# Index scores of two query blocks on ScalarE and GpSimd, weights' low parts in pieces, projection steps put first

## The chip, the cores and the metric

The kernel runs on one core of a Trainium2 chip. The metric is the device time of one execution in microseconds (us); the median of three runs of the kernel before is 1162.57 us (1162.12 to 1164.31). A difference below about 0.2%, some 2.3 us, can't be told from none.

## The reference

A trunk of two layers over 512 tokens of width 1024. Layer 0 mixes tokens with a sparse attention whose indexer picks keys (mixer A), layer 1 with a latent attention (mixer B); a squared-ReLU MLP follows each. Inputs and outputs are float32. What the change touches is mixer A's indexer:

```python
proj = h @ w_in                       # 16 heads of q, 4 of k and v, 8 index heads qi, one ki, weights wi
logits = einsum('bthd,bsd->bths', qib, ki)
score = einsum('bths,bth->bts', relu(logits), wib)   # sum over 8 index heads
score = where(visible, score, -inf)                  # chunks of 64, causal by chunk
_, sel = lax.top_k(score, 128)                       # keys that a query attends to
...                                                  # softmax attention of 16 heads over the selected keys
x = x + squared_relu_mlp(rms_norm(x), w_up, w_down)  # after each mixer; d_ff = 4096
```

## The kernel before

Every product of two float32 matrices is three TensorE passes on split numbers (a high part rounded to fp32r and a low part, the remainder): high by high, low by high, high by low, as `mm3` issues them (L227 to L229). So each weight tile is split before it is used. `Weights` keeps an ordered list of weight tiles ("items", mostly 128 partitions x 1024); `convert` fetches one with a DMA, makes the high part on ScalarE (L143, or on GpSimd at L141 for items marked "p" first) and the low part as raw minus high on GpSimd (L150, or on VectorE when so marked). MLP down weights go through L148 instead, which already works in pieces of 512 columns. Five items are held at a time, so a cast on ScalarE waits until TensorE is done with an item five earlier.

In mixer A, `idx_tile` projects the index queries and keys (`ip`, copied to `inat`), VectorE rotates 16 of every 64 columns (`rope`, L382, L384, L385) and scales the weights of heads (L741). `proj_tiles` is a generator of 32 steps, each three matmuls of 512 columns into a bank `pp`, that projects keys and values (`kv_done` copies them out on ScalarE and rotates on GpSimd) and then queries; `next(side)` puts one step between other work. After the index projection, TensorE transposes the rotated queries (`q_turn`, `qip`, L750) and keys (`kip`, L759), and these are split into `qis` and `ki`.

The index scores go over query blocks qb = 3, 2, 1 of 128 rows (block 0 needs no selection) with N = 512, 384, 256 keys, and for each over eight heads: one projection step, then two matmuls into a bank `lp` (L800, L801), then the sum over heads. Head 0 is max(x, 0) times its weight, straight from PSUM on VectorE (L804); heads 1 to 7 are a relu on ScalarE (L807) into one of two buffers and a multiply-add on VectorE into `bias` (L808). A memset masks the last chunk (L812). The scores of qb 3, 2, 1 stand in bias_120, bias_119, bias_118.

The selection (`rounds`) then takes 16 rounds per block on VectorE: MAX8 finds the eight largest (L777), MATCH_REPLACE8 marks them (L779), and at the end a compare turns marks into a mask of 0 and -1e30 (L781). Rounds of the blocks that are ready are taken in turn. The order of instructions on each engine is set by a scheduler from the written order and its own estimates; each engine then runs its list in order. The attention that follows adds `bias` to the scores in its row maximum on VectorE (L522).

In mixer B VectorE rotates the queries (L382, L384, L385 on `qn`, transposed by TensorE at L1021) while GpSimd makes both parts of the weights of later head groups (L141, L150).

## Time and profile before

| what | us |
|---|---|
| median of three runs | 1162.57 |
| the profiled execution's own time | 1162.26 |
| span of its trace | 1160.5 |
| TensorE busy (96% of the span) | 1116.6 |
| VectorE, ScalarE, GpSimd busy | 782.3, 604.3, 666.0 |

TensorE is busy nearly throughout, and its clock was granted in full but for a few stretches, so the time lies in the places where TensorE waits. They are in the first 16 us, in mixer A (to about 230 us), in mixer B (630 to 760 us) and in the last 10 us. Between these lie the two MLPs. A timeline row gives start, duration, engine, line, operation, output<-inputs and shape, and in brackets how long the engine had been idle and which instruction ended that.

### The profile page before, as it was taken

What the parts mean: (1) busy time and instruction counts of PE and PEld (TensorE: products, weight loads), DVE (VectorE), ACT (ScalarE), POOL (GpSimd) and SP (SyncE); (2) the same over time, 40 slices, a digit from 0 to 9 for tenths busy, and PEclk for the clock granted to TensorE, in tenths of its full rate; (3) what the DMA queues carried; (4) which work ended last, traced back from release to release, by engine and by line L of the source; (5) the groups of instructions that cost most, each with busy time, mean ns of one, the idle gap of its engine ahead of it and who ended that gap; (6) DMA issues with size and microseconds to landing.
All of it is one profiled execution on the core that took longest, in us unless ns stands there. A gap on an engine that the chain in (4) does not pass through costs nothing.

```text
span 1160.5 us, 15969 instructions
## 1 busy us (share of the span) xinstructions
PE 1116.6 (96%) x5721; PEld 949.8 (82%) x5721; DVE 782.3 (67%) x1419; ACT 604.3 (52%) x1115; POOL 666.0 (57%) x495
## 2 busy tenths in 40 slices
PE   6899899999999999999999899999999999999997
PEld 6778678879888888888889788888988888888886
DVE  7699998663566567566566888886556466556664
ACT  5453687654544554454445666563464454454452
POOL 4557433453657757856703642654457866856772
PEclk9999899999999999999999999999999999999999
DMA  6322100243124214313222200111414314412402
GB/s 210 111 64 86 67 1 2 72 135 103 63 83 145 91 55 145 127 55 110 80 66 79 75 31 25 55 55 55 164 56 145 109 56 126 146 56 90 145 12 80
DMA packets 65607, 99.56 MB, mean 86 GB/s; under 512 B 3188, under 2 KB 41848, under 8 KB 65528
## 3 DMA queue, kind: packets, MB, share of 16 engines
q1 hardware_dynamic: 65528, 98.55, 26.7%
q8 instruction: 45, 0.74, 0.3%
q14 instruction: 34, 0.28, 0.1%
HBM read 96.44 MB, written 2.10 MB: 85 GB/s over the span
## 4 chain that ended last, share of the span: by engine, by line
PE 79%; DVE 12%; issue 3%; ACT 3%; POOL 1%; DMA 1%; SPq 0%; DVEq 0%; POOLq 0%; ACTq 0%
PE dn L1144 22%; PE up L227 10%; PE up L228 10%; PE up L229 10%; PE s_ps L514 3%; PE o_ps L576 3%; PE wo_ps L227 2%; PE wo_ps L228 2%; PE wo_ps L229 2%; PE pt_ps L533 2%; DVE bias L779 2%; DVE m L777 2%; PE dn L228 1%; PE dn L229 1%; PE dn L227 1%
## 5 line engine op out<-in xcount | busy, mean ns | idle before, releaser
L148 POOL TENSOR_TENSOR w_lo<-quad,w_hi 128x512 fp32r<-128x512 f32 x196 | 275.0, 1433 | 162.9 <-ACT w_hi L143 160.3
L150 POOL TENSOR_TENSOR w_lo<-w_raw,w_hi 128x1024 fp32r<-128x1024 f32 (+4 forms) x117 | 265.0, 2284 | 89.0 <-ACT w_hi L143 88.6
L1147 DVE TENSOR_TENSOR x<-dn,x 128x512 f32<-128x512 f32 x196 | 135.0, 691 | 138.4 <-PE dn L1144 138.4
L228 PE MATMUL up<-hT_lo,w_hi 128*128 128x512 f32 (+1 forms) x576 | 210.5, 366 | 0.0
L227 PE MATMUL up<-hT_hi,w_hi 128*128 128x512 f32 (+1 forms) x576 | 209.3, 366 | 0.1
L229 PE MATMUL up<-hT_hi,w_lo 128*128 128x512 f32 (+1 forms) x576 | 208.5, 366 | 0.0
L143 ACT CAST w_hi<-w_raw 128x1024 fp32r<-128x1024 f32 (+6 forms) x108 | 109.3, 1020 | 154.9 <-PE dn L1144 61.9
L143 ACT CAST w_hi<-quad 128x1024 fp32r<-128x1024 f32 x98 | 101.2, 1051 | 99.4 <-DVE quad L86 71.8
L1144 PE MATMUL dn<-w_hi,lh 128*128 128x512 f32 x392 | 152.6, 389 | 0.2 <-ACT w_hi L143 0.2
L1144 PE MATMUL dn<-w_hi,ll 128*128 128x512 f32 x392 | 152.5, 389 | 0.0
L1144 PE MATMUL dn<-w_lo,lh 128*128 128x512 f32 x392 | 152.5, 389 | 0.0
L1109 DVE TENSOR_TENSOR ll<-u,lh 128x512 fp32r<-128x512 f32 x106 | 99.4, 968 | 40.8 <-ACT lh L1108 40.8
L228 PEld LDWEIGHTS up<-hT_lo,w_hi 128*128 128x128 f32 x576 | 108.6, 189 | 17.6 <-DVE hT_lo L428 0.2
L229 PEld LDWEIGHTS up<-hT_hi,w_lo 128*128 128x128 f32 x576 | 108.6, 189 | 17.5
L227 PEld LDWEIGHTS up<-hT_hi,w_hi 128*128 128x128 f32 x576 | 108.1, 189 | 17.7 <-ACT hT_hi L427 0.3
L86 DVE TENSOR_TENSOR quad<-quad 128x1024 f32<-128x1024 f32 x56 | 68.4, 1222 | 65.3 <-POOL w_lo L148 65.3
L1108 ACT CAST lh<-u 128x512 fp32r<-128x512 f32 x106 | 62.9, 621 | 76.3 <-DVE u L1121 67.9
L527 ACT ACTIVATE p<-p,m 128x128 f32<-128x128 f32 (+3 forms) x128 | 72.0, 563 | 32.5 <-DVE m L522 31.9
L1144 PEld LDWEIGHTS dn<-w_hi,lh 128*128 128x128 f32 x392 | 73.6, 188 | 15.7 <-issue 0.6
L1144 PEld LDWEIGHTS dn<-w_lo,lh 128*128 128x128 f32 x392 | 73.6, 188 | 15.3
L1144 PEld LDWEIGHTS dn<-w_hi,ll 128*128 128x128 f32 x392 | 73.6, 188 | 15.3
L619 POOL TENSOR_TENSOR oh<-o,ones 128x512 fp32r<-128x512 f32 x16 | 16.7, 1044 | 95.3 <-DVE o L613 65.3
(223 smaller groups left out, 2298.2 us busy)
## 6 DMA issues: line engine op xcount, KB each, us to landing
w_raw<-in_mlp_w_up_dram SPq DMA_DIRECT2D x64, 512.0 KB, 3.8
quad<-in_mlp_w_down_dram SPq DMA_DIRECT2D x56, 512.0 KB, 3.6
w_raw<-in_a_w_in_dram SPq DMA_DIRECT2D x12, 512.0 KB, 3.5
w_raw<-in_a_w_out_dram SPq DMA_DIRECT2D x8, 512.0 KB, 3.3
w_raw<-in_mlp_w_down_dram SPq DMA_DIRECT2D x8, 512.0 KB, 4.2
w_raw<-in_b_w_out_dram SPq DMA_DIRECT2D x8, 512.0 KB, 3.7
x<-in_x_dram SPq DMA_DIRECT2D x4, 512.0 KB, 7.1
w_raw<-in_b_w_kv_up_dram SPq DMA_DIRECT2D x4, 512.0 KB, 4.0
```

Of the source, the lines that this page charges most:

```text
L86: self.nc.vector.tensor_sub(q[o], q[l], q[r])
L143: nc.scalar.copy(h, v)
L148: nc.gpsimd.tensor_sub(l[:, cs], v[:, cs], h[:, cs].bitcast(F32))
L150: (nc.gpsimd if engs[1] == "p" else nc.vector).tensor_sub(l, v, h.bitcast(F32))
L227: nc.tensor.matmul(ps, lh, rh, start=first, stop=False)
L228: nc.tensor.matmul(ps, lh, rl, start=False, stop=False)
L229: nc.tensor.matmul(ps, ll, rh, start=False, stop=last)
L527: nc.scalar.activation(U["p"][:, :N], U["p"][:, :N], AF.Exp, bias=U["m"], scale=-1.0, accum_out=pair["sums"][:, c:c + 1])
L1108: nc.scalar.copy(lh, v)
L1109: nc.vector.tensor_sub(ll, v, lh.bitcast(F32))
L1144: nc.tensor.matmul(pp[t], l[:, k, ts], r[:, k, :], start=first and k == 0 and m == 0, stop=k == 1 and m == 2, skip_group_check=True)
L1147: last = nc.vector.tensor_add(x[:, cs], pp[t], x[:, cs])
```

## The change

Three edits, all in the functions shown above.

1. Low parts of weights that GpSimd makes from two-dimensional views are cut into equal pieces of at most 512 columns: 1024 becomes two of 512, 876 two of 438, 768 two of 384, 584 two of 292. The high parts, and the views by heads in mixer B, stay whole.
2. In the index scores, query block 3 stays as it was. For blocks 2 and 1 all eight heads take a relu on ScalarE and then a second ScalarE instruction that multiplies it by the head's weight; GpSimd adds the eight products (seven adds). The relu ring grows from two to four buffers.
3. Six projection steps (18 matmuls) are put ahead of the first transposes of rotated index queries and keys.

```diff
-            if callable(src):
-
-                for c in range(0, a * n, 512):
-                    cs = slice(c, c + 512)
+            if engs[1] == "p" and len(v.shape) == 2:
+
+                m = -(-a * n // 512)
+                for c in range(m):
+                    cs = slice(c * a * n // m, (c + 1) * a * n // m)
                     nc.gpsimd.tensor_sub(l[:, cs], v[:, cs], h[:, cs].bitcast(F32))
...
                     side = proj_tiles(f_b, kv_done)
+                    for _ in range(6):
+                        next(side)
...
-                            if h == 0:
+                            if h == 0 and qb == NT - 1:
                                 nc.vector.tensor_scalar(acc[qb], lp[:, :N], 0.0, wcol, op0=OP.max, op1=OP.mult)
                             else:
-                                r = pr.tile([P, 512], F32, name="relu", tag="relu", bufs=2)
+                                r = pr.tile([P, 512], F32, name="relu", tag="relu", bufs=4)
                                 nc.scalar.activation(r[:, :N], lp[:, :N], AF.Relu)
-                                nc.vector.scalar_tensor_tensor(acc[qb], r[:, :N], wcol, acc[qb],
-                                                               op0=OP.mult, op1=OP.add)
+                                if qb == NT - 1:
+                                    nc.vector.scalar_tensor_tensor(acc[qb], r[:, :N], wcol, acc[qb],
+                                                                   op0=OP.mult, op1=OP.add)
+                                else:
+                                    nc.scalar.activation(r[:, :N], r[:, :N], AF.Copy, scale=wcol)
+                                    if h == 0:
+                                        first = r
+                                    else:
+                                        nc.gpsimd.tensor_add(acc[qb], first[:, :N] if h == 1 else acc[qb], r[:, :N])
```

Lines of the changed file lie one to ten further down: L149 is the piece of a low part, L753 and L762 the transposes, L780 and L782 a round, L810 the relu, L815 the product with the weight, L819 the sum on GpSimd, L822 the memset. "waits" names the engines whose semaphores an instruction waits for.

TensorE at the transposes of the index queries and keys, before:

```order
L750 MATMUL qip<-ident,inat_127 128x128
L750 MATMUL qip<-ident,inat_128 128x128
L750 MATMUL qip<-ident,inat_129 128x128
L227 MATMUL pp<-w_hi,hT_hi 128x512
L228 MATMUL pp<-w_lo,hT_hi 128x512
L229 MATMUL pp<-w_hi,hT_lo 128x512
L759 MATMUL kip<-ident,inat_126 64x128
L759 MATMUL kip<-ident,inat_127 64x128
L759 MATMUL kip<-ident,inat_128 64x128
L759 MATMUL kip<-ident,inat_129 64x128
```

and after:

```order
L228 MATMUL pp<-w_hi,hT_hi 128x512
L229 MATMUL pp<-w_lo,hT_hi 128x512
L230 MATMUL pp<-w_hi,hT_lo 128x512
L753 MATMUL qip<-ident,inat_127 128x128
L753 MATMUL qip<-ident,inat_128 128x128
L753 MATMUL qip<-ident,inat_129 128x128
L228 MATMUL pp<-w_hi,hT_hi 128x512
L229 MATMUL pp<-w_lo,hT_hi 128x512
L230 MATMUL pp<-w_hi,hT_lo 128x512
L762 MATMUL kip<-ident,inat_126 64x128
L762 MATMUL kip<-ident,inat_127 64x128
L762 MATMUL kip<-ident,inat_128 64x128
```

Six steps of three matmuls, the last of which is shown, now stand ahead of the transposes.

VectorE where the scores of blocks 2 and 1 are summed, before (bias_119 is block 2, bias_118 block 1):

```order
L804 TENSOR_SCALAR bias_118<-lp,inat_127 128x256 [waits PE_49]
L777 MAX m_789<-bias_120 128x8 [waits DVE_49]
L808 SCALAR_TENSOR_TENSOR bias_119<-relu,inat_128,bias_119 128x384 [waits DVE_49,Activation_49]
L808 SCALAR_TENSOR_TENSOR bias_118<-relu,inat_127,bias_118 128x256 [waits DVE_49,Activation_49]
L779 MATCH_REPLACE bias_120<-m_789,bias_120 128x512 [waits DVE_49]
L812 MEMSET bias_119 64x64 [waits DVE_49]
L808 SCALAR_TENSOR_TENSOR bias_118<-relu,inat_127,bias_118 128x256 [waits DVE_49,Activation_49]
```

and after:

```order
L782 MATCH_REPLACE bias_120<-m_833,bias_120 128x512 [waits DVE_49]
L780 MAX m_867<-bias_120 128x8 [waits DVE_49]
L782 MATCH_REPLACE bias_120<-m_867,bias_120 128x512 [waits DVE_49]
L780 MAX m_901<-bias_120 128x8 [waits DVE_49]
L782 MATCH_REPLACE bias_120<-m_901,bias_120 128x512 [waits DVE_49]
L822 MEMSET bias_119 64x64 [waits Pool_49]
L780 MAX m_910<-bias_119 128x8 [waits DVE_49]
L780 MAX m_935<-bias_120 128x8
L782 MATCH_REPLACE bias_119<-m_910,bias_119 128x384 [waits DVE_49]
L782 MATCH_REPLACE bias_120<-m_935,bias_120 128x512 [waits DVE_49]
L780 MAX m_944<-bias_119 128x8 [waits DVE_49]
L780 MAX m_985<-bias_120 128x8 [waits DVE_49]
```

The multiply-adds of L808 are gone from VectorE's list, five rounds of bias_120 stand alone ahead of the memset of bias_119, and that memset now waits for GpSimd.

GpSimd at the same place, before (knat and vva are the keys and values that `kv_done` prepares):

```order
L382 TENSOR_TENSOR rope_v<-knat,ropeS_a 128x64 [waits Activation_49,Pool_49]
L384 TENSOR_TENSOR rope_u<-knat,ropeC_a 128x64
L385 TENSOR_TENSOR knat<-rope_u,rope_v 128x4x16 [waits Pool_49]
L150 TENSOR_TENSOR w_lo<-w_raw,w_hi 128x1024 [waits DMAHW4_49,PE_49,Activation_49]
L385 TENSOR_TENSOR knat<-rope_u,rope_v 128x4x16 [waits Pool_49]
L725 TENSOR_TENSOR vva<-v,vva 128x4x64 [waits Activation_49]
L726 TENSOR_TENSOR vva<-v,vva 128x64
L150 TENSOR_TENSOR w_lo<-w_raw,w_hi 128x1024 [waits DMAHW5_49,Activation_49]
L150 TENSOR_TENSOR w_lo<-w_raw,w_hi 128x1024 [waits DMAHW6_49,Activation_49]
L150 TENSOR_TENSOR w_lo<-w_raw,w_hi 128x1024 [waits DMAHW7_49,Activation_49]
```

and after:

```order
L726 TENSOR_TENSOR vva<-v,vva 128x4x64 [waits Activation_49]
L727 TENSOR_TENSOR vva<-v,vva 128x64
L819 TENSOR_TENSOR bias_119<-bias_119,relu 128x384 [waits Pool_49]
L386 TENSOR_TENSOR knat<-rope_u,rope_v 128x4x16 [waits Pool_49]
L819 TENSOR_TENSOR bias_119<-bias_119,relu 128x384 [waits Pool_49]
L819 TENSOR_TENSOR bias_118<-relu 128x256 [waits Activation_49]
L819 TENSOR_TENSOR bias_119<-bias_119,relu 128x384 [waits Pool_49]
L819 TENSOR_TENSOR bias_118<-bias_118,relu 128x256 [waits Activation_49,Pool_49] x3
L149 TENSOR_TENSOR w_lo<-w_raw,w_hi 128x512 [waits DMAHW5_49,Activation_49]
L149 TENSOR_TENSOR w_lo<-w_raw,w_hi 128x512
L819 TENSOR_TENSOR bias_118<-bias_118,relu 128x256 [waits Activation_49,Pool_49] x3
```

The sums of bias_119 and bias_118 now stand in GpSimd's list among the work on keys and values and among the pieces of the weights' low parts.

ScalarE at the last heads of block 1, before:

```order
L807 ACTIVATE relu<-lp 128x256 [waits DVE_49]
L143 CAST w_hi<-w_raw 128x1024 [waits DMAHW4_49]
L724 CAST vva<-v 128x4x64 [waits Activation_49]
L807 ACTIVATE relu<-lp 128x256 [waits DVE_49,PE_49] x2
L143 CAST w_hi<-w_raw 128x1024 [waits DMAHW5_49,PE_49]
L143 CAST w_hi<-w_raw 128x1024 [waits DMAHW6_49,PE_49]
```

and after:

```order
L810 ACTIVATE relu<-lp 128x256 [waits PE_49,Pool_49]
L815 ACTIVATE relu<-relu,inat_127 128x256 [waits Activation_49]
L810 ACTIVATE relu<-lp 128x256 [waits PE_49]
L815 ACTIVATE relu<-relu,inat_127 128x256 [waits Activation_49]
L143 CAST w_hi<-w_raw 128x1024 [waits DMAHW5_49,PE_49]
L810 ACTIVATE relu<-lp 128x256 [waits PE_49,Pool_49] x2
L815 ACTIVATE relu<-relu,inat_127 128x256 [waits Activation_49] x2
L810 ACTIVATE relu<-lp 128x256 [waits PE_49,Pool_49]
```

The cast of the next weight item, which waits for TensorE (PE) to release a buffer, stood behind all relus and now stands ahead of the last three.

## Rows read from the trace of the kernel before

**Rows 1.** The page: busy time, share of the span, instructions of each engine.

```profile
PE 1116.6 (96%) x5721; PEld 949.8 (82%) x5721; DVE 782.3 (67%) x1419; ACT 604.3 (52%) x1115; POOL 666.0 (57%) x495
```

**Rows 2.** Windows: stretch, length, busy (count) of PE, PEld, DVE, ACT, POOL; clock, DMA, GB/s.

```profile
30.00:60.00 30.00, 26.66 (x155) 23.35 (x154) 18.28 (x31) 14.46 (x25) 14.52 (x7) 0.94 0.43 123
74.70:86.05 11.35, 10.74 (x53) 8.82 (x52) 11.35 (x25) 6.09 (x17) 11.31 (x22) 1.00 0.19 50
120.00:150.00 30.00, 24.58 (x142) 21.34 (x141) 27.27 (x82) 21.71 (x59) 15.19 (x19) 0.89 0.11 36
259.00:588.00 329.00, 328.76 (x1551) 275.65 (x1549) 194.58 (x231) 156.75 (x211) 215.39 (x134) 1.00 0.31 97
```

**Rows 3.** Timeline of TensorE in mixer A; start, us, operation, tile, wait.

```profile
44.66 0.60 PE L759 MATMUL kip<-ident,inat 128*64 128x128 f32 x4 [3.34 <-DVE inat L385]
...
62.22 0.39 PE L801 MATMUL lp<-ki,qis 128*128 128x512 f32 x1
...
131.57 1.54 PE L514 MATMUL s_ps<-k,qs 128*128 128x512 f32 x4 [5.42 <-DVE m L522]
```

**Rows 4.** Chain that ended last, a piece in the first MLP.

```profile
306.43 13.60 PE dn L1144 x60
```

**Rows 5.** Timeline of VectorE in mixer A.

```profile
42.31 2.20 DVE L385 TENSOR_TENSOR inat<-rope_u,rope_v 128x16 f32<-128x16 f32 x1
...
62.66 3.36 DVE L808 SCALAR_TENSOR_TENSOR bias<-relu,inat,bias 128x512 f32<-128x512 f32 x2 [0.93 <-ACT relu L807]
...
66.64 0.70 DVE L777 MAX8 m<-bias 128x8 f32<-128x512 f32 x1
...
89.14 0.11 DVE L812 MEMSET bias<- 64x64 f32 x1
...
98.18 1.47 DVE L777 MAX8 m<-bias 128x8 f32<-128x256 f32 x3
...
101.14 1.47 DVE L777 MAX8 m<-bias 128x8 f32<-128x256 f32 x3
...
128.76 2.17 DVE L781 TENSOR_SCALAR bias<-bias 128x256 f32<-128x256 f32 x1
...
132.02 0.69 DVE L855 TENSOR_TENSOR qs<-qT,qs 64x512 fp32r<-64x512 f32 x1
```

**Rows 6.** Timeline of GpSimd in mixer A.

```profile
39.78 7.03 POOL L150 TENSOR_TENSOR w_lo<-w_raw,w_hi 128x1024 fp32r<-128x1024 f32 x3 [4.17 <-ACT w_hi L143]
...
128.44 2.35 POOL L150 TENSOR_TENSOR w_lo<-w_raw,w_hi 128x1024 fp32r<-128x1024 f32 x1
```

**Rows 7.** GpSimd's groups by line and form: count, busy us, mean ns, idle before.

```profile
L150 POOL TENSOR_TENSOR w_lo<-w_raw,w_hi 128x1024 fp32r<-128x1024 f32 x100 | 239.8, 2417 | 79.2 <-ACT w_hi L143 78.8
...
L150 POOL TENSOR_TENSOR w_lo<-w_raw,w_hi 128x512 fp32r<-128x512 f32 x6 | 7.7, 1304 | 0.0
...
L725 POOL TENSOR_TENSOR vva<-v,vva 128x256 fp32r<-128x256 f32 x4 | 3.2, 799 | 0.0
L150 POOL TENSOR_TENSOR w_lo<-w_raw,w_hi 128x384 fp32r<-128x384 f32 x3 | 3.1, 1028 | 0.0
```

**Rows 8.** Timeline of ScalarE, the cast of a weight item.

```profile
71.14 1.05 ACT L143 CAST w_hi<-w_raw 128x1024 fp32r<-128x1024 f32 x1 [0.25 <-PE pp L229]
```

**Rows 9.** Timeline of TensorE in mixer B: three waits.

```profile
691.98 0.66 PE L533 MATMUL pt_ps<-ident,p 128*128 128x128 f32 x4 [1.25 <-DVE pt_lo L549]
...
742.32 0.64 PE L1021 MATMUL qbT<-ident,qn 128*96 128x128 f32 x4 [1.39 <-DVE o L613]
...
757.25 0.32 PE L1021 MATMUL qbT<-ident,qn 128*96 128x128 f32 x1 [0.82 <-DVE qn L385]
```

**Rows 10.** Timeline of VectorE in mixer B, two rotations.

```profile
689.24 2.35 DVE L385 TENSOR_TENSOR qn<-rope_u,rope_v 128x128 f32<-128x128 f32 x1
...
739.14 2.46 DVE L384 TENSOR_TENSOR rope_u<-qn,ropeC_b 128x128 f32<-128x128 f32 x1
```

**Rows 11.** Timeline of GpSimd in mixer B, the low parts beside the second.

```profile
736.69 4.76 POOL L150 TENSOR_TENSOR w_lo<-w_raw,w_hi 128x1024 fp32r<-128x1024 f32 x2
```

## The prediction

> **What bounds the kernel now.** I read the page's busy line first: TensorE works in 96% of the span [rows 1]. In the MLPs it is saturated, 328.76 of 329.00 us with the clock granted in full, 2.4 GHz [rows 2], so nothing that GpSimd or VectorE does there moves the end unless it gets later than its slack. The change must be read where TensorE waits. Of the larger waits three kinds are touched: 3.34 us ahead of the key transposes, with the clock at 0.94 in the stretch around it [rows 2, 3]; 5.42 us at the start of the attention, where the selection on VectorE ends last, with 0.89 [rows 2, 3]; and small ones in mixer B [rows 9]. From 66.64, where the first round starts [rows 5], to 130.93, where the last compare ends [rows 5], VectorE has no gap to speak of: that selection is the chain that sets the attention's start.
>
> Next I laid VectorE's rows against GpSimd's. L385 on 16 columns takes 2.20 us at 42.31 [rows 5] beside three low parts of 2.34 each that started at 39.78 [rows 6]; it ends at 44.51, about where the second of them ends (44.47). L781 ends at 130.93, GpSimd's piece beside it at 130.79 [rows 5, 6]; the L808 pair at 62.66 takes 3.36 us, where two passes over 512 columns make 1.4 (0.70 each by the MAX8 at 66.64). So a VectorE instruction with two SBUF inputs, or this compare, that starts while GpSimd works waits for the end of GpSimd's instruction. MAX8 and MATCH_REPLACE8 keep their times beside GpSimd, 1.47 for three MAX8 at 98.18 and at 101.14 alike [rows 5].
>
> **Six steps ahead.** Eighteen matmuls at 0.227 us (13.60 us for 60 [rows 4]) make 4.1 us and fill the 3.34 us wait. The key transposes start at 41.3 + 4.1 = 45.4, 0.75 us later, with six steps done. The clock lost in 30 to 60 us is at most 0.06 x 30 = 1.8 us [rows 2]; mostly regained, the last score matmul of block 3 ends at 61.6 and not 62.45 [rows 3]. Each head of block 2 takes three matmuls of 512 columns and two of 384, 3 x 0.227 + 2 x 0.17 = 1.02 to 1.04, so block 2 ends at 61.6 + 8.3 = 69.9. On TensorE this part gains about 5 us, but it had 5.42 us of waiting for VectorE further on: the gain counts only as far as the selection ends earlier.
>
> **Scores to ScalarE and GpSimd.** VectorE loses 16 instructions of some 0.5 us (384 or 256 columns at 1.47 for 1152 [rows 5], and an entry), about 8 us, but its list now stops for GpSimd. Block 3 is summed at 61.6 + relu, hand-over and sum = 63.1. Then only five rounds of it stand ahead of the memset of bias_119, at 0.70 + 0.08 + 0.67, near 1.5 [rows 5]: VectorE is idle from 70.7.
>
> GpSimd's list has no gap from 65.9 on (block 3's last relu until 62.3, a cast 1.05 [rows 8], the low part in two pieces 2.6): seven sums of 384 columns at 1.03 (the nearest two-input row of that width [rows 7]) 7.2; one of 256 columns 0.80 [rows 7]; the work on keys and values, 11.31 busy in 74.70 to 86.05 [rows 2] less a low part of 2.40, 8.9; one item in two pieces of 1.30 [rows 7], 2.6. That is 19.5: bias_119 comes at 85, and VectorE has stood still for over 14 us. The price of a sum isn't in the trace; between 0.5 (VectorE's pass over that width) and 1.30 (a 512 piece) I take the row of equal width.
>
> The Trainium skill gives another price ("GPSIMD Engine Reference", section "Performance versus the Vector engine"): about 2.6 cycles an element for two inputs. At the 1.2 GHz that it reckons with, 384 elements would be an estimated 0.83 us, and bias_119 1.4 us earlier; the row of 1.03 speaks for the longer time, as it holds the fixed part too.
>
> From 85, three rounds of block 2 and two of block 3 keep VectorE to 90.5 (a round of all three blocks is 101.14 - 98.18 = 2.96 [rows 5]; without block 1's 0.75 it is 2.2; 2 x 2.2 + 1.05). Then the memset of bias_118 waits. On ScalarE the cast of the next weight item stands ahead of its last three relus, and that cast waits for TensorE: 75 matmuls after block 2 x 0.227 = 17.0, five heads' scores 1.2, the key transposes 0.4, so 69.9 + 18.6 = 88.5. Cast 1.05 [rows 8], two pieces 2.6, three sums of 256 columns 2.3: bias_118 at 94.5. Before it stood at 89.14 [rows 5], with as many rounds of each block left in both lists. So the selection is **5.4 us later** there. From this goes the stretched compare at 128.76, 2.17 where a pass over 256 columns takes 0.3 [rows 5], now beside a piece half as long or none: -1.9. Three or four instructions for the attention (two qs at 0.69 [rows 5], one k, one pt_lo: 2.2) move ahead of the end of the selection and are not lost, since they stood behind it. The selection ends near 136.5, and what follows it shifts by 5.4 - 1.9 = 3.5, with the hand-over **+3.6 us**. TensorE runs out of work near 119 and waits for all of it. Bounds: +1.5, if GpSimd's sums go at 0.8 and TensorE reaches the release 1 us earlier; +5.5, if the 1.9 isn't regained or relus waiting for a buffer hold up TensorE's score banks.
>
> **Pieces.** Each of 100 low parts of 128 x 1024 costs 2 x 1.30 - 2.42 = 0.2 us more [rows 7]. GpSimd's slack in the MLPs hides it; if it were gone each item would cost 0.2 us, but GpSimd is busy in 215 of 329 us [rows 2]. I take +0.2 for the edges. In mixer B the pieces shorten what a rotation waits for. L384 at 739.14 takes 2.46 us [rows 10] beside the second of two low parts from 736.69 [rows 11]; L385 at 689.24 takes 2.35 [rows 10] beside one. With half the hold they end 1.05 to 2 us earlier, and TensorE's waits of 1.25, 1.39 and 0.82 [rows 9] shrink by 1.05, 1.39 and 0.8. With 0.4 at the stage's start that is **-3.65 us**. Not shown is whether a VectorE instruction gets in between two pieces at once or after the second; hence from 0 (it never does) to -5 (with clock regained). GpSimd's high parts (L141) and the views by heads stay whole, so I stay away from the far end.
>
> **Sum.** 1162.26 + 3.6 - 3.65 + 0.2 = 1162.4 for the profiled execution; the median of the runs shown lies 0.3 us higher. The front part can give back a little or not (0 to 0.3). I say **1162.8 us**, no change.
>
> **Rivals.**
> (a) Slower, 1166: pieces don't help rotations. GpSimd starts its next piece before VectorE gets in, so L384 waits for two pieces as for one low part. For it: the L385 at 42.31 ended with the low part beside it, not sooner, and GpSimd went on at once with the next. Against: that L385 started at 42.31, after the first low part's end at 42.12, so the L384 ahead of it, with two SBUF inputs as well, had been let in between. Mixer B then gains under 1 us, and 1162.6 + 3.6 = 1166.2 stands. It decides from a relief under 1.2 us.
> (b) Faster, 1158.5: B's relief is 5 us with its clock, and TensorE reaches the release sooner, so that bias_118 comes at 92.4: 1162.6 + 1.5 - 5 = 1159, with the front part 1158.5.
> (c) Faster, 1149: the sums are ready when VectorE needs them. 16 rounds x 2.96 = 47.4 us of selection [rows 5] from 66 plus the few instructions between give an end at 117, TensorE's own work at 119.5 decides, and 131.57 - 119.5 = 12 us go. Against it stands GpSimd's list of 19.5 us ahead of bias_119. The Trainium skill names such an offload as worth a try when VectorE is saturated, and warns in the same place that GpSimd and VectorE share a read port, so that moving work between those two might not help ("Perfetto Trace Analysis", section "Optimizing Scalar/DVE Operations"). By its first half this rival would hold, by its second the forecast; the stretched L385 agrees with the second.
>
> **How the numbers follow.** Forecast 0.46 (1160.3 to 1165.0), (a) 0.28, (b) 0.20, (c) 0.06. The range leaves out (c) and the tails of (a) and (b): 1157.5 to 1167.5. Within 0.2%, 2.3 us (what a measurement of this kernel can tell from none), lies the forecast's own range and little else: same 0.45; faster (b) and (c) 0.26; slower (a) and what the forecast spills 0.29.
>
> **What would show it.** Right: no wait at the key transposes and full clock in 30 to 60; no L808 of over 1 us; VectorE idle from about 71 to 85 with bias_119's memset ended by GpSimd, and again for some 4 us ahead of bias_118; the selection's last compare ending at 135 to 138; TensorE waiting some 15 us there; pieces of 1.30; in mixer B rotations of at most 1.5 us and 3 to 4 us less waiting. Wrong: bias_119 before 80, or sums much under 0.8 (then (c) or (b)); rotations as long as before (then (a)); or a wait of TensorE inside the score stage that pushes its own end past VectorE's.

## The result and the profile after

The changed kernel takes 1175.1 us (median; 1173.41 to 1176.54) against 1162.34 for the kernel before on the same chip: a ratio of 1.0105 [1.0093, 1.0117]. It is 1.05% slower, where no change was forecast, and the time lies above the range given. The profiled execution took 1175.99 us with a span of 1174.2, so 13.7 us of span are to be explained. The page's busy line of the changed kernel:

```profile
PE 1117.2 (95%) x5721; PEld 948.9 (81%) x5721; DVE 776.2 (66%) x1403; ACT 611.2 (52%) x1133; POOL 695.7 (59%) x617
```

Against [rows 1] TensorE's work is the same to 0.6 us. VectorE gave up 6.1 us and GpSimd took on 29.7, so in sum the 13.7 us are waits of TensorE, not work. To find them I took the same TensorE instruction in both traces and subtracted the starts; the table holds this shift for the changed kernel at seven places.

| place (start before) | shift, us | step from the row above |
|---|---|---|
| key transposes (44.66) | +0.1 | |
| first scores of block 3 (53.9) | -1.0 | -1.1 |
| attention after the selection (140 to 220) | +8.8 | +9.8 |
| first MLP (270) | +15.0 | +6.2 |
| start of mixer B (594) | +15.6 | +0.6 |
| end of mixer B, second MLP's start (820) | +12.4 | -3.2 |
| end of the span | +13.7 | +1.3 |

The filled wait comes first, in TensorE's timeline and in two windows of the changed kernel (columns as in [rows 2] and [rows 3]):

```profile
44.78 0.60 PE L762 MATMUL kip<-ident,inat 128*64 128x128 f32 x4
```

```profile
30.00:60.00 30.00, 29.75 (x173) 25.81 (x172) 17.43 (x31) 15.24 (x26) 18.14 (x14) 1.00 0.47 136
...
124.00:144.00 20.00, 6.33 (x23) 4.73 (x24) 18.30 (x51) 4.92 (x14) 4.74 (x9) 0.50 0.08 27
```

The wait of 3.34 us ahead of the key transposes is gone and the clock is full from 30 to 60 (0.94 before). Against that, at the end of the selection TensorE works 6.33 of 20 us, with 0.50 of its clock. VectorE's timeline says what it waits for; L822 is the memset that closes a block's scores, L784 the compare at the end of a selection:

```profile
83.51 0.11 DVE L822 MEMSET bias<- 64x64 f32 x1 [12.71 <-POOL bias L819]
...
95.32 0.11 DVE L822 MEMSET bias<- 64x64 f32 x1 [5.96 <-POOL bias L819]
...
124.02 2.93 DVE L784 TENSOR_SCALAR bias<-bias 128x512 f32<-128x512 f32 x1
...
140.19 0.29 DVE L784 TENSOR_SCALAR bias<-bias 128x256 f32<-128x256 f32 x1
```

VectorE, which had no gap to speak of here before, stands still for 12.71 and 5.96 us until GpSimd's sums are there, and the last compare ends at 140.48 and not at 130.93. The three rows that lead to the second of these memsets, ScalarE's cast and GpSimd's two pieces and last three sums behind it, are those that the forecast named:

```profile
89.24 1.05 ACT L143 CAST w_hi<-w_raw 128x1024 fp32r<-128x1024 f32 x1 [1.38 <-PE pp L230]
```

```profile
90.37 2.55 POOL L149 TENSOR_TENSOR w_lo<-w_raw,w_hi 128x512 fp32r<-128x512 f32 x2 [1.62 <-ACT w_hi L143]
...
92.87 2.37 POOL L819 TENSOR_TENSOR bias<-bias,relu 128x256 f32<-128x256 f32 x3
```

TensorE stands behind VectorE (L865 makes qs, L523 is the row maximum):

```profile
122.38 1.12 PE L515 MATMUL s_ps<-k,qs 128*128 128x128 f32 x4 [2.72 <-DVE qs L865]
...
127.82 1.09 PE L859 MATMUL qT<-ident,qnat 128*128 128x128 f32 x4 [2.44 <-DVE qs L865]
...
133.21 1.03 PE L836 MATMUL kT<-ident,knat 128*64 128x128 f32 x4 [4.30 <-DVE qs L865]
...
141.00 1.54 PE L515 MATMUL s_ps<-k,qs 128*128 128x512 f32 x4 [6.77 <-DVE m L523]
```

The row at 141.00 answers to that at 131.57 in [rows 3]: four long waits, 16.2 us in all, where one of 5.42 stood.

The second place is the output projection of mixer A. There TensorE waits for GpSimd, and GpSimd's timeline shows why: pieces of the MLP's weights stand ahead of and between the two copies that the projection needs (L620 makes the high part oh of the attention's output, L623 the low part ol).

```profile
256.92 0.50 PE L228 MATMUL wo_ps<-w_hi,oh 128*128 128x512 f32 x1 [1.59 <-POOL oh L620]
...
260.63 1.20 PE L230 MATMUL wo_ps<-w_hi,ol 128*128 128x512 f32 x4 [1.57 <-POOL ol L623]
```

```profile
253.34 2.53 POOL L149 TENSOR_TENSOR w_lo<-w_raw,w_hi 128x512 fp32r<-128x512 f32 x2 [8.04 <-ACT w_hi L143]
255.84 1.03 POOL L620 TENSOR_TENSOR oh<-o,ones 128x512 fp32r<-128x512 f32 x1
256.83 2.52 POOL L149 TENSOR_TENSOR w_lo<-w_raw,w_hi 128x512 fp32r<-128x512 f32 x2
259.32 1.25 POOL L623 TENSOR_TENSOR ol<-o,oh 128x512 fp32r<-128x512 f32 x1
```

Before, oh, ol and then both whole low parts followed one another, at 244.08, 245.20 and 246.46. Behind the two waits TensorE's clock is lower for a while, which a window shows (0.50 again from 273.4 to 276; before, the clock was 1.00 all through this stretch):

```profile
262.00:266.00 4.00, 4.00 (x11) 3.14 (x12) 2.41 (x5) 2.30 (x4) 0.55 (x1) 0.57 0.93 330
```

Its matmuls of 512 columns start 0.43 us apart there and not 0.23. Of the 6.2 us of this step in the table, the two waits are 3.2 and the lower clock some 2.5. Third, mixer B gains as much as the forecast said, and VectorE's two rotations that answer to 737.14 and 739.14 (2.08 us, and 2.46 [rows 10]) are shorter:

```profile
751.77 0.98 DVE L383 TENSOR_TENSOR rope_v<-qn,ropeS_b 128x128 f32<-128x128 f32 x1
752.67 1.37 DVE L385 TENSOR_TENSOR rope_u<-qn,ropeC_b 128x128 f32<-128x128 f32 x1
```

Fourth, the end of the second MLP has a wait that was not there before:

```profile
1134.33 0.47 PE L1154 MATMUL dn<-w_hi,lh 128*128 128x512 f32 x1 [0.82 <-ACT w_hi L143]
```

### The profile page after: what moved, and what is told of

It is laid out like the page before. It is cut to its first block, busy times and chain, and to the rows that moved or that the text cites. A ratio compares the mean times of both kernels' runs of the same rounds, so it can differ in the third digit from the quotient of the medians.

```text
span 1174.2 us, 16100 instructions
## 1 busy us (share of the span) xinstructions
PE 1117.2 (95%) x5721; PEld 948.9 (81%) x5721; DVE 776.2 (66%) x1403; ACT 611.2 (52%) x1133; POOL 695.7 (59%) x617
## 4 chain that ended last, share of the span: by engine, by line
PE 78%; DVE 10%; POOL 4%; issue 4%; ACT 3%; DMA 1%; SPq 0%; POOLq 0%; DVEq 0%; ACTq 0%
PE dn L1154 21%; PE up L228 9%; PE up L229 9%; PE up L230 9%; PE s_ps L515 3%; POOL w_lo L149 3%; PE o_ps L577 3%; PE pt_ps L534 2%; PE wo_ps L230 2%; PE wo_ps L228 2%; PE wo_ps L229 2%; DVE bias L782 2%; DVE m L780 1%; PE tps L424 1%; PE dn L228 1%
## 5 line engine op out<-in xcount | busy, mean ns | idle before, releaser
L149 POOL TENSOR_TENSOR w_lo<-quad,w_hi 128x512 fp32r<-128x512 f32 x196 | 272.9, 1422 | 159.6 <-ACT w_hi L143 157.1
L149 POOL TENSOR_TENSOR w_lo<-w_raw,w_hi 128x512 fp32r<-128x512 f32 (+3 forms) x219 | 279.0, 1305 | 71.2 <-ACT w_hi L143 70.4
L1119 DVE TENSOR_TENSOR ll<-u,lh 128x512 fp32r<-128x512 f32 x106 | 106.4, 1034 | 45.3 <-ACT lh L1118 45.3
L547 ACT CAST pt_hi<-pt_ps 128x128 fp32r<-128x128 f32 (+3 forms) x128 | 53.2, 424 | 32.9 <-PE pt_ps L534 31.4
```

The lines of the kernel that those rows point to most:

```text
L149: nc.gpsimd.tensor_sub(l[:, cs], v[:, cs], h[:, cs].bitcast(F32))
L547: nc.scalar.copy(view(H["hi"]), U["src"])
L1119: nc.vector.tensor_sub(ll, v, lh.bitcast(F32))
```

## The experiments

All ratios are to the kernel before on the same chip, in brackets the 95% interval. "Attention" is the shift of TensorE's instructions behind the selection (before: 135 to 145), "end" that of the span's end.

### Each part alone

**e1_pieces**: the pieces, without the other two parts.

```diff
-            if callable(src):
+            if engs[1] == "p" and len(v.shape) == 2:
...
-                for c in range(0, a * n, 512):
-                    cs = slice(c, c + 512)
+                m = -(-a * n // 512)
+                for c in range(m):
+                    cs = slice(c * a * n // m, (c + 1) * a * n // m)
```

> Low parts in pieces alone; scores and projection steps as before. The loss of the changed kernel lies in three places of its trace: the start of the attention (+8.8 us), the output projection of mixer A, where pieces stand between the two copies oh and ol (+5), and the MLPs' ends (+2); mixer B gives 3.5 back. Theory: the first comes from the scores on GpSimd, the other three from the pieces. Then this kernel gains up to 2 us at the attention's start (last compare not held), loses 5 in the projection and 2 in the MLPs, gains 3.5 in mixer B: 1163 to 1166. Rival: the pieces cause the start's delay too, as GpSimd is fuller and holds VectorE for longer stretches: 1170 or more. Second rival: the relief in mixer B belongs to the other parts: 1167 to 1169.

Measured: 1160.32 us, 0.9988 [0.9979, 0.9997]. Attention -7.0, first MLP -1.9, mixer B's end -3.4, end -0.7. As a whole this can't be told from no change. By the shifts the pieces help at the start of the attention, by far more than the 1.9 us of one compare that the forecast gave them there, and lose most of it in the output projection. The timelines of GpSimd and TensorE in this kernel show the same order as in the changed one:

```profile
241.39 1.03 POOL L620 TENSOR_TENSOR oh<-o,ones 128x512 fp32r<-128x512 f32 x1
242.38 2.53 POOL L149 TENSOR_TENSOR w_lo<-w_raw,w_hi 128x512 fp32r<-128x512 f32 x2
244.88 1.26 POOL L623 TENSOR_TENSOR ol<-o,oh 128x512 fp32r<-128x512 f32 x1
```

```profile
242.47 0.50 PE L228 MATMUL wo_ps<-w_hi,oh 128*128 128x512 f32 x1 [1.60 <-POOL oh L620]
...
246.19 1.19 PE L230 MATMUL wo_ps<-w_hi,ol 128*128 128x512 f32 x4 [1.58 <-POOL ol L623]
```

Nothing of GpSimd's sums or of the steps is in this kernel, so the pieces are the cause of these two waits. The key transposes' wait also fell from 3.34 to 1.25 us, and the selection's three compares took 0.50, 0.34 and 0.68 us, where the last alone had taken 2.17 [rows 5].

**e2_scores**: the sums of blocks 2 and 1 on ScalarE and GpSimd alone.

```diff
+                                    nc.scalar.activation(r[:, :N], r[:, :N], AF.Copy, scale=wcol)
+                                    if h == 0:
+                                        first = r
+                                    else:
+                                        nc.gpsimd.tensor_add(acc[qb], first[:, :N] if h == 1 else acc[qb], r[:, :N])
```

> Scores of blocks 2 and 1 on ScalarE and GpSimd alone; low parts whole, no steps ahead. Theory: VectorE stands idle for GpSimd's sums, 10 us or more in two stretches, and the attention starts 7 to 10 us later; mixer B and the MLPs as before: 1169 to 1173. Rival: with whole low parts and without the six steps GpSimd's list isn't behind, and the delay is under 3 us: 1162 to 1165.

Measured: 1169.41 us, 1.0065 [1.0052, 1.0077]. Attention +2.1, first MLP +7.7, end +6.3. VectorE's timeline holds the two waits for GpSimd (L816 is the sum here):

```profile
78.69 0.11 DVE L819 MEMSET bias<- 64x64 f32 x1 [5.37 <-POOL bias L816]
...
90.61 0.11 DVE L819 MEMSET bias<- 64x64 f32 x1 [6.08 <-POOL bias L816]
```

With the steps and the pieces left out, block 2 is 4.8 us earlier than in the changed kernel and block 1 4.7 us. The offload alone slows the kernel. Only 2.1 of it comes from the later selection; the other 5.6 us, between there and the MLP, come with a different order of the attention's instructions, whose shifts vary by several us either way. At least 1.8 of them stand at its far end, in the timelines of TensorE and VectorE (L395 scales the rows that the MLP's transposes wait for):

```profile
264.04 1.94 PE L423 MATMUL tps<-ident,h 128*128 128x128 f32 x8 [3.73 <-DVE h L395]
```

```profile
261.07 3.49 DVE L395 SCALAR_TENSOR_TENSOR h<-x,rs_y,gain 128x512 f32<-128x512 f32 x2
```

The wait was 1.90 us before, and the pair took 1.41; here it starts beside a whole low part on GpSimd (2.35 us from 261.00). No run here takes the rest apart.

**e3_steps**: the six steps alone.

```diff
                     side = proj_tiles(f_b, kv_done)
+                    for _ in range(6):
+                        next(side)
```

> Six projection steps ahead alone. Theory: TensorE's wait of 3.34 us at the key transposes goes, scores start about 1 us earlier, but the selection on VectorE sets the attention's start, so the gain is 0.5 to 1.5 us and TensorE waits 8 to 9 us there instead of 5.42: 1161 to 1162. Rival: the steps gain what they fill, 3 to 5 us: 1157 to 1159.

Measured: 1174.00 us, 1.0100 [1.0085, 1.0114]: nearly the whole loss, with no sum on GpSimd. Attention +7.1, first MLP +12.7 (here too the attention's order is another one), end +11.8. Nor is the wait at the key transposes filled: they start at 47.19, behind a wait of 1.56 us. VectorE's timeline at the sums of block 1, all on VectorE in this kernel:

```profile
88.31 1.07 DVE L810 SCALAR_TENSOR_TENSOR bias<-relu,inat,bias 128x256 f32<-128x256 f32 x2 [2.61 <-ACT relu L809]
...
93.20 3.62 DVE L810 SCALAR_TENSOR_TENSOR bias<-relu,inat,bias 128x256 f32<-128x256 f32 x2 [3.82 <-ACT relu L809]
96.89 0.11 DVE L814 MEMSET bias<- 64x64 f32 x1
```

The memset of bias_118 comes at 96.89, 7.75 us later than in [rows 5], and what is waited for is a relu, thus TensorE's scores. TensorE's timeline shows every fourth of the sixteen score matmuls of block 1:

```profile
76.72 0.28 PE L802 MATMUL lp<-ki,qis 128*128 128x256 f32 x1
...
82.42 0.28 PE L802 MATMUL lp<-ki,qis 128*128 128x256 f32 x1
...
87.45 0.28 PE L802 MATMUL lp<-ki,qis 128*128 128x256 f32 x1
...
91.59 0.28 PE L802 MATMUL lp<-ki,qis 128*128 128x256 f32 x1
```

Before, these heads ran from 72.99 to 85.11; here they come in pairs some 5 us apart and end at 92.23. Of the 32 steps of `proj_tiles` one stands ahead of the keys, the splitting of the queries takes eight and 23 of the 24 heads one each. The six used early are missing in block 1, and where its heads have no step of their own the scheduler puts some fifteen to twenty later projection matmuls between two pairs. This is the largest cause of the late selection.

### Pairs

**e4_pieces_steps**: both without the sums.

```diff
+            if engs[1] == "p" and len(v.shape) == 2:
...
+                    for _ in range(6):
+                        next(side)
```

> Pieces and steps without the scores' move. In this kernel's list on GpSimd the copies oh and ol of the last head group stand ahead of the pieces again, as in the kernel before. Theory: 1 to 3 us gained at the attention's start, nothing lost in the projection, 3.5 gained in mixer B, up to 2 lost in the MLPs: 1157 to 1161, faster than before. Rival: the projection's loss comes from the pieces' longer time and not from their place in the list: 1162 to 1165.

Measured: 1174.38 us, 1.0103 [1.0087, 1.0119]. Block 1's scores end at 88.95, bias_118 comes at 92.77. Attention +6.8, first MLP +11.6, end +9.8. That would bring the selection's end 4 us ahead of e3_steps, but a compare takes it back (0.40 us in e3_steps), in the timelines of VectorE and TensorE:

```profile
120.51 4.61 DVE L784 TENSOR_SCALAR bias<-bias 128x512 f32<-128x512 f32 x1
```

```profile
126.75 2.13 PE L515 MATMUL s_ps<-k,qs 128*128 128x128 f32 x6 [8.90 <-DVE qs L858]
```

**e9_pieces_scores**: pieces and sums, without the steps.

```diff
+            if engs[1] == "p" and len(v.shape) == 2:
...
+                                    nc.scalar.activation(r[:, :N], r[:, :N], AF.Copy, scale=wcol)
```

> Pieces and scores without the six steps. With pieces alone the attention starts 6.5 us earlier than before, with scores alone 3 us later (and more is lost inside that attention). Theory: each part does here what it does alone, bias_118 comes at 85 to 89 and not at 95 as in the changed kernel, so the attention starts within 3 us of the kernel before; with the projection's loss of 4 to 6 us behind it, 1164 to 1168. Rival: the sums, not the steps, make the changed kernel's delay of 8.8 us: bias_118 at 93 or later, 1172 or more.

Measured: 1167.58 us, 1.0056 [1.0042, 1.0071]. Bias_118 comes at 89.43, 0.3 us later than in the kernel before. Attention +0.8, rising to +2.3, first MLP +5.9, end +5.7. Against e1_pieces (-7.0) the sums cost 7.8 us at the start of the attention; against the changed kernel (+8.8) the steps cost 8.0 there. From e4_pieces_steps (+6.8) to the changed kernel the sums add only 2.0: both parts delay the same thing, bias_118, and whichever comes second adds little.

### The steps without their later cost

**e6_steps_from_head**: the six steps early, taken from the loop that splits the queries (hp), which uses eight of the 32; it keeps two, and the 24 heads keep theirs.

```diff
+                    for _ in range(6):
+                        next(side)
...
-                            next(side, None)
+                            if hp == 3:
+                                next(side, None)
```

> Six projection steps ahead, taken out of the eight between the transposes of the index queries and not out of the last heads' scores; low parts whole, scores on VectorE. With the steps ahead alone (1174.0) the last eight heads had no step left between them, TensorE's list put them among later projections, and block 1's scores ended at 92.2 instead of 85.1. In this kernel's list they stand where they stood before. Theory: the scores end by 86, the loss of 12 us goes: 1158 to 1163. Rival: the six steps are harmful where they are put (GpSimd and ScalarE get their weights late): 1168 or more.

Measured: 1162.78 us, 1.0009 [1.0000, 1.0018]. Block 1's scores end at 86.14, 1.0 us later than before, the attention stays within +0.3 to +1.8, the end at -0.3. So the loss of e3_steps is the missing steps. There is no gain either, and TensorE's timeline says why (L752 transposes queries, L774 splits them):

```profile
45.31 0.60 PE L761 MATMUL kip<-ident,inat 128*64 128x128 f32 x4
...
49.27 0.52 PE L752 MATMUL qip<-ident,inat 128*128 128x128 f32 x3 [3.02 <-DVE qis L774]
50.95 0.68 PE L752 MATMUL qip<-ident,inat 128*128 128x128 f32 x3 [1.17 <-DVE qis L774]
```

The 3.34 us of wait at the keys are gone and stand 4 us further on as 3.02 and 1.17: from the keys to the first score ScalarE and VectorE split the queries, 9.3 us before (44.66 to 53.92) and 9.7 here. The steps that lay beside that work now lie ahead of it, and what fills the first wait can't shorten it.

**e8_all_from_head**: the whole change with its steps taken so.

```diff
+                            if hp == 3:
+                                next(side, None)
```

> The whole change, but the six steps taken from the head, so that the last heads' scores keep their steps. Theory (steps): TensorE's list and not GpSimd's sums made block 1's scores late in the changed kernel; here they end by 87 and the attention starts 4 us or more earlier than in the changed kernel: 1165 to 1170. Rival (sums): GpSimd's list of sums, keys and pieces sets bias_118 as before, at 94 to 96: 1173 to 1176.

Measured: 1171.86 us, 1.0087 [1.0073, 1.0101]. Attention +4.3 where the change has +8.8, so half of the loss there is the missing steps, in the company of the sums: bias_118 comes at 92.67, 2.65 us earlier than in the changed kernel, and the compare of 512 columns takes 0.40 us and not 2.93. Later it is +10.6, by the order of the attention and the projection, and the end +11.4.

### Pieces where they help

**e5_pieces_limited**: pieces for mixer A's input weights (i < 18) and the weights of mixer B marked "p" first, whole low parts for the rest (the MLPs' down weights stay in the pieces that they had).

```diff
-            if callable(src):
+            if engs[1] == "p" and len(v.shape) == 2 and (i < 18 or engs[0] == "p" or callable(src)):
```

> Pieces for mixer A's input weights and mixer B's alone; low parts of the output weights of mixer A and of the MLPs whole again; scores and steps as before. With all pieces the start of the attention came 7.0 us earlier and mixer B gave 1.8, but 5.1 were lost between the attention and the first MLP and 2.7 at the last MLP's end. Theory: these losses come from the pieces of the output and MLP weights, which stood between the copies oh and ol in GpSimd's list; here they don't. Then 7 to 9 us are gained: 1153 to 1156. Rival: the front's gain is swallowed further on in any case, because TensorE then waits for something that didn't get earlier: 1159 to 1162.

Measured: **1155.90 us, 0.9948 [0.9935, 0.9961]**, faster than both kernels. Attention -4.8, the same in the output projection, -3.9 in the first MLP, mixer B's end and the span's end both -6.4. GpSimd's timeline at the projection has the old order, and TensorE waits for neither copy:

```profile
239.26 1.04 POOL L620 TENSOR_TENSOR oh<-o,ones 128x512 fp32r<-128x512 f32 x1 [8.53 <-DVE o L614]
240.38 1.30 POOL L623 TENSOR_TENSOR ol<-o,oh 128x512 fp32r<-128x512 f32 x1
241.65 4.77 POOL L151 TENSOR_TENSOR w_lo<-w_raw,w_hi 128x1024 fp32r<-128x1024 f32 x2
```

With e10_all_limited below this shows the cause of the 6.2 and the last 1.3 us of the change: the pieces of the output and MLP weights.

**e10_all_limited**: the whole change with the pieces limited so.

```diff
+            if engs[1] == "p" and len(v.shape) == 2 and (i < 18 or engs[0] == "p" or callable(src)):
...
+                    for _ in range(6):
+                        next(side)
```

> The whole change, but with pieces for mixer A's input weights and mixer B's alone. Theory: of the changed kernel's loss the 6.2 us between the attention and the first MLP and the 1.6 us at the last MLP's end come from pieces of the output and MLP weights; here oh and ol stand ahead of the low parts, so 1175.1 falls by 6 to 8: 1167 to 1169. Rival: the late selection shifts the lists in any case and the copies wait elsewhere: 1172 or more.

Measured: 1167.55 us, 1.0053 [1.0040, 1.0066]. Attention +5.6, rising to +7.1; +7.1 still in the first MLP, no wait for oh or ol; end +4.6. The 6.2 us of the projection are gone in the presence of the other parts too, and what stays is the late selection.

**e7_best**: limited pieces and steps from the splitting loop, the two parts that did no harm, together.

```diff
+            if engs[1] == "p" and len(v.shape) == 2 and (i < 18 or engs[0] == "p" or callable(src)):
...
+                            if hp == 3:
+                                next(side, None)
```

> The limited pieces and the six steps taken from the head together, scores on VectorE. Theory: the steps fill the rest of the wait at the key transposes (1.25 us with pieces alone) and its lost clock, so 0.5 to 2 us on top of the limited pieces, if the selection on VectorE starts earlier by that: 1152 to 1155. Rival: selection and not TensorE sets the attention's start, nothing on top: 1154 to 1157, as the limited pieces alone.

Measured: 1158.97 us, 0.9976 [0.9966, 0.9986], 3 us slower than e5_pieces_limited. The key transposes start at 44.3 with the steps and at 42.03 without. With a wait of only 1.25 us left there, 4.1 us of steps delay the keys by more than they fill.

**e11_pieces_22**: four more items in pieces, up to i < 22.

```diff
-            if engs[1] == "p" and len(v.shape) == 2 and (i < 18 or engs[0] == "p" or callable(src)):
+            if engs[1] == "p" and len(v.shape) == 2 and (i < 22 or engs[0] == "p" or callable(src)):
```

> Limited pieces, extended to the first four items of mixer A's output weights, which GpSimd splits beside the end of the selection; scores and steps as before. With limited pieces (1155.9) the last compare took 2.16 us beside a whole low part, with all pieces 0.68. In this kernel's list oh and ol stay ahead of the low parts. Theory: 1.3 to 1.5 us more at the attention's start, and somewhat of its lost clock: 1153.5 to 1155. Rival: TensorE isn't waiting for the compare alone, nothing more: 1155.5 to 1156.5.

Measured: 1156.16 us, 0.9950 [0.9938, 0.9962], the same as with 18. The theory that the last compare of e5_pieces_limited (2.16 us, beside a whole low part) could be shortened for a gain of 1.3 to 1.5 us fell: it still took 1.77.

### How long GpSimd holds a VectorE instruction

**e12_hold**: a kernel of its own, in which VectorE's compare of 512 columns, or an add of two SBUF inputs, starts while GpSimd works through a list of equal instructions.

```diff
+        for k in range(n):
+            nc.gpsimd.tensor_sub(d[i][:, :cols] if k == 0 else g[:, k], last[:, :cols], c[:, :cols])
+        if form == "compare":
+            nc.vector.tensor_scalar(e[i], d[i], -3.2e38, NEG, op0=OP.is_gt, op1=OP.mult)
+        else:
+            nc.vector.tensor_add(e[i][:, :128], d[i][:, :128], c[:, :128])
```

> Not the reference's computation: eight stretches in which GpSimd runs 12 subtractions of 128x128 or 6 of 128x512 without a gap, and VectorE, released by the first, does one compare of 128x512 (one input) or one addition of 128x128 (two inputs), each twice. Theory (one instruction): each VectorE instruction ends a fraction of a us after the GpSimd instruction that runs when it is ready: up to 0.9 us beside 128x128, up to 1.7 beside 128x512. Rival (until idle), as the changed kernel's compare of 2.93 us suggests: the compare ends after GpSimd's last instruction of the stretch, 5 us or more beside 128x128 and 6 or more beside 128x512, and the addition gets in after one instruction.

Measured, in VectorE's timeline: straight behind VectorE's own memset, then released by GpSimd beside its instructions of 512 columns, and of 128.

```profile
10.50 0.36 DVE L76 TENSOR_SCALAR e<-d 128x512 f32<-128x512 f32 x1
...
20.52 1.47 DVE L76 TENSOR_SCALAR e<-d 128x512 f32<-128x512 f32 x1 [6.63 <-POOL d L74]
...
37.27 0.66 DVE L76 TENSOR_SCALAR e<-d 128x512 f32<-128x512 f32 x1 [6.57 <-POOL d L74]
```

The first compare isn't held although GpSimd's list runs beside it; there GpSimd loses, and its eleven instructions take 5.59 us and not 4.64. Against it the compare is 1.1 us longer beside instructions of 1.26 us, and 0.3 us longer beside those of 0.45; the list ran on for four and ten more of them. It waits for the one that runs, at most, and not until GpSimd is idle. For an instruction of VectorE in a mode that uses two ports the Trainium skill says the same ("SBUF — State Buffer", section "Who interferes with whom"): who issues first has the shared port pair for its whole instruction, and the other is blocked. These rows agree.

**e13_hold_rope**: the same with the rotation's strided instructions on GpSimd and the compare in place, to look for the 2.93 us of the changed kernel.

```diff
+            nc.gpsimd.tensor_tensor(u[k], straight, cs, op=OP.mult)
+            if k % 2:
+                for m in (k - 1, k):
+                    nc.gpsimd.tensor_add(straight, u[m], v[m])
```

> Not the reference's computation: six stretches in which GpSimd runs low parts of 128x512 and the rotation's instructions of 128x128 (eight heads of 16 columns, read with a stride of 64) back to back, and VectorE does one compare of 128x512 in place, as the selection's last step does. Theory (the rotation's form or the write in place keeps VectorE out): beside rotations the compare lasts until GpSimd's list stops, 2 us or more. Rival (one instruction): beside rotations 0.6 to 0.9 us, beside low parts at most 1.7; then the 2.93 us of the changed kernel and the 4.61 of pieces with steps come from something that these stretches don't hold.

Measured in VectorE's timeline, beside low parts and beside rotations:

```profile
5.70 1.47 DVE L99 TENSOR_SCALAR bias<-bias 128x512 f32<-128x512 f32 x1 [0.25 <-POOL bias L92]
...
38.50 0.66 DVE L99 TENSOR_SCALAR bias<-bias 128x512 f32<-128x512 f32 x1 [7.04 <-POOL bias L92]
```

One instruction again. The form of the rotations isn't what makes the hold long.

## Why the prediction was wrong

**The steps that failed.** The forecast added three terms. The gain in mixer B held: -3.65, measured -3.5. The late selection, +3.6, measured +8.8, and the pieces elsewhere, +0.2, measured +8.1; these two make 13.1 of the 13.6 us by which the profiled execution missed its sum. So what failed is, first, "GpSimd's slack in the MLPs hides it", and second, the way from bias_118 to the attention. The price of the six steps was wrong as well, but their cost was in the sum under another name.

**Steps: priced at nothing, and counted elsewhere.** "On TensorE this part gains about 5 us ... the gain counts only as far as the selection ends earlier" gave the part a floor of nothing. It followed the six steps to where they went and not to where they were taken from. Alone the part costs 11.8 us of span, 7.1 of it at the start of the attention (e3_steps); with the steps taken from the splitting of the queries it costs nothing, and gains nothing, since the splitting of the queries is the bound behind the wait (e6_steps_from_head). But the forecast had read the 75 matmuls between block 2 and the release of the cast in TensorE's list, 17.0 us, and so had the late heads in its time of bias_118.

**Sums: times and chain right, cause half wrong.** Bias_119 was forecast at 85 and came at 83.51, bias_118 at 94.5 and came at 95.32, and the cast ahead of it at 88.5 and came at 89.24; a sum of 384 columns at 1.03 measured 1.02 to 1.03. VectorE idled 12.7 us and 6.0, where over 14 and some 4 were foreseen. But the delay of bias_118 was put down to the cast and the sums, and what made the cast late is the steps: with pieces and sums and no steps it comes at 83.18 and bias_118 at 89.43 (e9_pieces_scores), and with steps and no sum on GpSimd bias_118 comes at 96.89 (e3_steps). The estimate that the prediction worked out from the Trainium skill ("GPSIMD Engine Reference"), 0.83 us a sum, is short of the rows, 1.02.

**From bias_118 to the attention: +3.6 became +8.8.** Of the 5.2 us between, 0.8 are bias_118. About 2.5 are the compare of 512 columns at 124.02, 2.93 us where 0.41 stood before: the forecast took the hold of the last compare away (-1.9, and it took 0.29 as foreseen) and did not see another come at the end of a different block. Some 1.6 are the 2.2 us of work moved ahead that "are not lost": behind the selection the shift falls only from +9.4 to +8.8, while TensorE comes out of 20 us at half its clock. These three make 4.9; 0.3 stays unplaced. That the lower clock is what kept the 1.6 from being regained is argued and not shown.

**Pieces: +0.2 became 6.2 + 0.6 + 1.3 us.** "GpSimd's slack in the MLPs hides it" asked only whether GpSimd has time, not what else is in its list. At the edge between attention and MLP the pieces changed its order, oh, pieces, ol in place of oh, ol, low parts, and TensorE waited twice, 1.59 and 1.57 us; limited pieces take the whole step away (e5_pieces_limited, e10_all_limited). Some 2.5 us more went in the lower clock behind the waits; in e1_pieces the same two waits came without it (1.00 from 247.5 to 252) and cost less, so what decides that is open. The same edit gains 7.0 us at the start of the attention when alone, through the keys' wait, the holds and the clock, of which the sum credited 1.9 for the last compare.

**Mixer B: -3.65, measured -3.5** at its lowest. The wait of 1.25 us [rows 9] went as priced. Of the other two the price was too high: they go, but new waits stand behind them, 0.38 and 1.13 us (0.19 before) behind the one, 0.91 (0.20 before) behind the other. The waits together gave about 2.0. The other 1.5 us are a stretch of lower clock (0.79 from 757 to 765 before) that e6_steps_from_head, without any piece in mixer B, escapes too. So the total is right in part by luck: some two fifths of it are not in its working.

**Rivals.** (a) fell: rotations are 1.1 us shorter, 2.08 and 2.46 against 0.98 and 1.37. Its sign was right for another reason. (c) fell with e2_scores: the sums are late, as the row of 1.03 said, and offloading to GpSimd did not help. (b)'s gain in mixer B was not reached. None of the three held the order at the projection or the hold of another compare, so the range was too narrow above.

**What isn't settled.** Why another 5 to 6 us go between the start of the attention and the MLP in e2_scores, e3_steps, e4_pieces_steps and e8_all_from_head: the attention's instructions stand in another order in all four, and up to the projection in the old order in every other kernel here, but no run fixed that order, and only the 1.8 us at the far end (e2_scores) are placed. And the long holds, below.

## What to carry to other kernels

A step moved forward as a filler is missing where it stood: read the list at both ends, and ask whether what is behind the filled wait is bound by another engine. Cutting an instruction for one wait is good there and can change the order of a list elsewhere, so cut only where a wait ends on it (here -6.4 us instead of -0.7). Two edits that delay the same late tile don't add up (the parts alone gave -0.1%, +0.65% and +1.00%, all three +1.05%), so single experiments bound a sum and don't make it.

## What the runs showed of the hardware

The compare of 512 columns took 2.93 us in the changed kernel and 4.61 us in e4_pieces_steps, beside a run of back-to-back GpSimd instructions. In GpSimd's timeline of the changed kernel this run is

```profile
123.30 0.90 POOL L386 TENSOR_TENSOR qnat<-rope_u,rope_v 128x128 f32<-128x128 f32 x2
124.12 0.49 POOL L383 TENSOR_TENSOR rope_v<-qnat,ropeS_a 128x128 f32<-128x128 f32 x1
...
125.77 0.90 POOL L386 TENSOR_TENSOR qnat<-rope_u,rope_v 128x128 f32<-128x128 f32 x2
```

It ends at 126.67, and the compare at 126.95: the hold lasted over seven instructions of some 0.5 us, until GpSimd had nothing left. In e4_pieces_steps it lasted over nine and in e10_all_limited over three (1.40 us), each time until the last of a run. In e12_hold and e13_hold_rope the same compare waited for one. There VectorE had been released by GpSimd's semaphore, while in the changed kernel the compare followed other work on VectorE. That alone doesn't make the difference: the last compares of the kernel before (128.76 [rows 5, 6]) and of e5_pieces_limited (124.89, 2.16 us) also followed other work, and were held by one low part, though a rotation stood right behind it. What decides is open; the section of the Trainium skill named above knows only the hold by one instruction, and 2.93 and 4.61 don't fit it.

GpSimd's time for two inputs was 0.45 us for 128 columns and 1.26 for 512 (e12_hold), 0.75 for 256 and 1.02 for 384 (the changed kernel), so a part of some 0.2 us doesn't shrink with the width. And TensorE's clock was granted at 0.50, the lower of its two levels (1.2 GHz), all through the stretch from 124 to 144 in which it worked in short groups between waits, so a stretch of waits costs more than their sum.
